# Small constant tiles allocated before the activation tile in a two-layer hybrid decoder trunk

## The chip, the core and the metric

The kernel runs on one core of one Trainium2 chip. The metric is device time in microseconds (us), the median of several executions of the same program. The times below come from one profiled execution where they carry a place in the program, and from three timed runs where they are called runs.

## What is computed

Two residual layers over 512 tokens of width 1024, all in float32. Layer 0 mixes tokens with gated linear attention and block-sparse softmax attention, layer 1 with a gated short convolution and multi-scale pooling. Each layer ends in a wide squared-ReLU MLP, and most of the arithmetic is in the projections and in these two MLPs:

```
def mlp(h, w1, w2):
    a = jax.nn.relu(h @ w1)          # 512x1024 @ 1024x4096
    return (a * a) @ w2              # 512x4096 @ 4096x1024

def reference(x, ...):
    for i in range(DEPTH):           # DEPTH = 2
        h = rmsnorm(x, norm_mix[i])
        x = x + (mix_even(h, ...) if i % 2 == 0 else mix_odd(h, ...))
        h = rmsnorm(x, norm_mlp[i])
        x = x + mlp(h, w1[i], w2[i])
    return x
```

## The kernel before

Channels lie on the 128 partitions, and the 512 tokens run along the free axis of every activation tile. Every large product is done three times: an operand is split into a high and a low part (float32r), and helper `mm3` (lines 124 to 129) issues hi by hi, hi by lo and lo by hi into the same PSUM tile. One such matmul has a stationary operand of 128x128, loaded by its own weight load (PEld in the profile), and a moving operand of 128x512.

Weights arrive as 184 blocks of 128x1024 (512 KB). `block_parts` (lines 101 to 113) fetches a block by SyncE's DMA queue into `raw`, ScalarE casts it to `whi` (line 111), VectorE subtracts to get `wlo` (line 112). The pool `wp` holds four blocks, and three are made ahead of their use. A block feeds 24 matmuls.

Tile `A` (128 partitions, 32 rows of 512 float32r, so 2,048 bytes a row) holds activations: rows 0 to 7 and 8 to 15 the high and low parts of the normed input (called H), rows 16 to 23 and 24 to 31 those of a mixer's output or of an MLP quarter (called O). `t_unit` (lines 131 to 156) reads rows of `A` as the moving operand and weights as the stationary one; the units called qa, ka, ra, wob, woa, u, cg, xc, bg, wo and m1 (all shown as `m<-A` in the MLP) are of this kind. `tok_g` (lines 158 to 172; units kb, qb, vb, va) swaps them: columns of `A` are stationary, weights move.

The MLP (lines 301 to 376) makes its 4096 hidden rows in four quarters of 1024. The quarters 0 and 2 are stored in `A` rows 16 to 31, the quarters 1 and 3 in a tile `E` of 16 rows, which lives in a pool of its own (line 304). `m2(g)` multiplies quarter g by w2, always at line 360 through the same `mm3`, so it reads `A` for g = 0 and 2 and `E` for g = 1 and 3. The order is m1(0), m1(1), m2(0), m1(2), m2(1), m1(3), m2(2), m2(3). One m1(g) or one m2(g) is 4 units x 2 blocks x 24 = 192 matmuls, except the last unit of the program, which is cut finer (lines 332 to 343).

The order of TensorE's work is the order in which the code issues it; in the attention stage of layer 0 a small planner (class `Plan`) interleaves attention steps with pieces of projections by costs written into the kernel. Neither depends on where a tile lies.

The order in which tiles are asked of a pool sets where they lie in a partition. The pool `cp` is opened first (line 60) and its tiles follow each other, rounded up to 32 bytes. The pools behind it start where it ends. These are the byte offsets within a partition that the compiled program has, and their remainders modulo 2,048:

| tile | offset | remainder |
|---|---|---|
| kk, later x | 16,512 | 128 |
| A | 32,896 | 128 |
| cn, vc, g2, eps_c, one_c, ones_r, warm | 98,432 to 106,432 | 128, 1920, 128, 1152, 1184, 1216, 1728 |
| raw, whi, wlo (blocks of 4,096 bytes) | 106,432 to 147,392 | 1984 |
| E | 155,584 | 1984 |
| pwh (pooling weights) | 157,632 | 1984 |
| ph (pooled inputs) | 178,432 and up | 256 |

Of the kernel before, what the change touches and what calls it, by code (L numbers as in the profile page):

```python
# [8 lines left out]
F32R = mybir.dt.float32r  # L9
# [5 lines left out]
P = 128  # L15
S = 512
KT = 8
# [27 lines left out]
def kernel(  # L45
# [14 lines left out]
    cp = ctx.enter_context(tc.tile_pool(name="cp", bufs=1))  # L60
# [4 lines left out]
    )  # L65

    x = None
    kk = cp.tile([P, KT, S], F32R, tag="x", name="kk")
    A = cp.tile([P, 32, S], F32R, name="A")
    cn = cp.tile([P, C_N], F32, name="cn")  # L70
    vc = cp.tile([P, V_N], F32, name="vc")
    g2 = cp.tile([97, 256], F32, name="g2")
# [5 lines left out]
    ones_r = cp.tile([P, P], F32R, name="ones_r")  # L78
    warm = cp.tile([P, 64], F32, name="warm")
    dve.memset(warm, 0.0)  # L80
    ident = cn[:, C_ID : C_ID + P]
    ones = cn[:, C_ONE : C_ONE + P]
    dist = cn[:, C_DIST : C_DIST + S]
# [4 lines left out]
    def col(i, n=1):  # L88
        return vc[:, i : i + n]
# [34 lines left out]
    def mm3(o, w_hi, w_lo, a_hi, a_lo, start, stop, swap=False):  # L124
        if swap:
            w_hi, w_lo, a_hi, a_lo = a_hi, a_lo, w_hi, w_lo
        pe.matmul(o, w_hi, a_hi, start=start, stop=False)  # L127
        pe.matmul(o, w_hi, a_lo, start=False, stop=False)  # L128
        pe.matmul(o, w_lo, a_hi, start=False, stop=stop)  # L129

    def t_unit_g(name, acts):
        o = mm_tile(name)
        n = len(acts)
        for b in range(n // 4):
# [3 lines left out]
            for kk in range(4):  # L138
                k = b * 4 + kk
                for j in range(2):  # L140
                    c = slice(j * P, (j + 1) * P)
                    mm3(o[:, j, :], hi[:, kk, c], lo[:, kk, c], A[:, acts[k][0], :], A[:, acts[k][1], :],
                        k == 0, k == n - 1)
# [14 lines left out]
    def tok_g(name, evac):  # L158
        blocks = []
        for half in range(2):  # L160
            o = mm_tile(f"{name}{half}")
            for k in range(KT):
# [4 lines left out]
                for j in range(2):  # L167
                    t = slice((2 * half + j) * P, (2 * half + j + 1) * P)
                    mm3(o[:, j, :], hi[:, c], lo[:, c], A[:, k, t], A[:, 8 + k, t], k == 0, k == KT - 1, swap=True)
                if k == KT - 1:  # L170
# [1 line left out]
                yield  # L172

    class Plan:
        """Orders the tensor engine's steps: the first listed step whose inputs are due, else a piece of the filler."""

        def __init__(self, banks):
            self.free = {t: [0.0] * n for t, n in banks.items()}
# [76 lines left out]
    def split_h(k, gcol, src, c=slice(0, S)):  # L255
        act.activation(A[:, k, c], src[:, k, c], AF.Copy, scale=col(gcol + k))
        dve.scalar_tensor_tensor(  # L257
            A[:, 8 + k, c], src[:, k, c], col(gcol + k), A[:, k, c].bitcast(F32), op0=ALU.mult, op1=ALU.subtract
        )
# [41 lines left out]
    def mlp(l, nrm, nxt):  # L301
        with ExitStack() as c2:
# [4 lines left out]
            def aslot(f):  # L307
                i = f % 8
                if (f // 8) % 2 == 0:
                    return A[:, 16 + i, :], A[:, 24 + i, :]  # L310
                return E[:, i, :], E[:, 8 + i, :]

            def apair(f):
                i = f % 8
                if (f // 8) % 2 == 0:
                    return A[:, 16 + i : 18 + i, :], A[:, 24 + i : 26 + i, :]
                return E[:, i : i + 2, :], E[:, 8 + i : 10 + i, :]
# [736 lines left out]
```

## Time and profile before

| | |
|---|---|
| three runs | 1119.59, 1121.35, 1121.45 us (median 1121.35) |
| span of the profiled execution | 1119.5 us |
| TensorE matmuls (PE) | 1109.4 us busy, 99%, 5008 matmuls |
| TensorE weight loads (PEld) | 891.2 us, 80% |
| VectorE (DVE) | 556.7 us, 50% |
| ScalarE (ACT) | 405.1 us, 36% |
| GpSimd (POOL) | 103.1 us, 9% |
| mean traffic to and from memory | 93 GB/s |

The profiled execution's own device time is not given beside its span. The span runs from the first to the last instruction; the lowest run is 0.09 us above it and the median 1.85 us. The busy time of PE is no measure of work: matmuls are pipelined, and each record (about 0.39 us) overlaps the next. The time from the start of one matmul to the start of the next is what counts, and it is read from the timeline, where rows carry their start.

### The profile page before, as it was taken

What the parts mean: (1) busy time and instruction counts of PE and PEld (TensorE: products, weight loads), DVE (VectorE), ACT (ScalarE), POOL (GpSimd) and SP (SyncE); (2) the same over time, 40 slices, a digit from 0 to 9 for tenths busy, and PEclk for the clock granted to TensorE, in tenths of its full rate; (3) what the DMA queues carried; (4) which work ended last, traced back from release to release, by engine and by line L of the source; (5) the groups of instructions that cost most, each with busy time, mean ns of one, the idle gap of its engine ahead of it and who ended that gap; (6) DMA issues with size and microseconds to landing.
All of it is one profiled execution on the core that took longest, in us unless ns stands there. A gap on an engine that the chain in (4) does not pass through costs nothing.

```text
span 1119.5 us, 12567 instructions
## 1 busy us (share of the span) xinstructions
PE 1109.4 (99%) x5008; PEld 891.2 (80%) x5008; DVE 556.7 (50%) x774; ACT 405.1 (36%) x554; POOL 103.1 (9%) x110
## 2 busy tenths in 40 slices
PE   9999999999999999999999999999999999999998
PEld 7777778678888888888888888888888888888887
DVE  6887765758544334334325674455443334334321
ACT  5564455535433123223214332244433133133110
POOL 2132312214000000000002100021000000000000
PEclk9999999999999999999999999999999999999999
DMA  7222114113222222223223222232233322232331
GB/s 225 76 76 95 57 43 147 58 57 96 93 95 94 94 94 94 95 96 97 91 100 102 88 94 95 95 94 94 94 94 94 95 94 95 95 94 94 94 112 57
DMA packets 32043, 104.84 MB, mean 94 GB/s; under 512 B 3729, under 2 KB 6258, under 8 KB 31986
## 3 DMA queue, kind: packets, MB, share of 16 engines
q1 hardware_dynamic: 31202, 101.69, 28.0%
q0 software_dynamic: 640, 2.10, 0.6%
q8 instruction: 39, 0.64, 0.2%
q10 hardware_dynamic: 144, 0.26, 0.1%
q14 instruction: 18, 0.15, 0.0%
HBM read 101.94 MB, written 2.10 MB: 93 GB/s over the span
## 4 chain that ended last, share of the span: by engine, by line
PE 93%; DVE 3%; ACT 1%; DMA 1%; POOL 1%; issue 1%; SPq 0%; POOLq 0%; DVEq 0%
PE m L127 21%; PE m L129 21%; PE m L128 21%; PE wo L127 1%; PE wo L129 1%; PE wo L128 1%; DMA raw<-in_w_dram 1%; PE av L690 1%; PE s L642 1%; PE ptp L671 1%; PE s L641 1%; PE va L127 1%; PE cg L129 1%; PE bg L127 1%; PE woa L129 1%; PE woa L128 1%
## 5 line engine op out<-in xcount | busy, mean ns | idle before, releaser
L111 ACT CAST whi<-raw 128x1024 fp32r<-128x1024 f32 (+1 forms) x188 | 193.8, 1031 | 557.6 <-PE m L128 448.0
L112 DVE TENSOR_TENSOR wlo<-raw,whi 128x1024 fp32r<-128x1024 f32 (+1 forms) x188 | 227.7, 1212 | 210.2 <-ACT whi L111 209.9
L128 PE MATMUL m<-A,whi 128*128 128x512 f32 x768 | 303.4, 395 | 0.0
L129 PE MATMUL m<-A,wlo 128*128 128x512 f32 x768 | 303.4, 395 | 0.0
L127 PE MATMUL m<-A,whi 128*128 128x512 f32 x768 | 303.4, 395 | 0.0
L129 PEld LDWEIGHTS m<-A,wlo 128*128 128x128 f32 x768 | 144.1, 188 | 35.1
L128 PEld LDWEIGHTS m<-A,whi 128*128 128x128 f32 x768 | 144.1, 188 | 35.1
L127 PEld LDWEIGHTS m<-A,whi 128*128 128x128 f32 x768 | 144.1, 188 | 35.0
L128 PE MATMUL m<-E,whi 128*128 128x512 f32 (+1 forms) x264 | 101.0, 383 | 0.0
L127 PE MATMUL m<-E,whi 128*128 128x512 f32 (+1 forms) x264 | 101.0, 383 | 0.0
L129 PE MATMUL m<-E,wlo 128*128 128x512 f32 (+1 forms) x264 | 101.0, 383 | 0.0
L287 DVE TENSOR_TENSOR x<-x,m 128x1024 f32<-128x1024 f32 x31 | 37.9, 1222 | 111.9 <-PE m L129 111.9
L326 DVE SCALAR_TENSOR_TENSOR r<-m,rs_n 128x1024 f32<-128x1024 f32 x32 | 39.2, 1225 | 102.3 <-PE m L129 102.3
L268 POOL TENSOR_TENSOR ss_n<-ss_n,sq_n 128x512 f32<-128x512 f32 x21 | 32.8, 1564 | 401.7 <-ACT sq_n L266 401.0
L127 PEld LDWEIGHTS m<-E,whi 128*128 128x128 f32 x264 | 49.6, 188 | 9.8
L129 PEld LDWEIGHTS m<-E,wlo 128*128 128x128 f32 x264 | 49.6, 188 | 9.8
L128 PEld LDWEIGHTS m<-E,whi 128*128 128x128 f32 x264 | 49.6, 188 | 9.7
L327 ACT ACTIVATE r<-r 128x1024 f32<-128x1024 f32 x32 | 34.0, 1063 | 20.3 <-DVE r L326 20.3
L330 DVE TENSOR_TENSOR E<-r,E 128x1024 fp32r<-128x1024 f32 x16 | 19.6, 1225 | 17.2 <-ACT E L329 17.2
L257 DVE SCALAR_TENSOR_TENSOR A<-x,vc,A 128x512 fp32r<-128x512 f32 x24 | 27.3, 1142 | 1.2
L330 DVE TENSOR_TENSOR A<-r,A 128x1024 fp32r<-128x1024 f32 x16 | 19.6, 1224 | 15.1 <-ACT A L329 15.1
L127 PE MATMUL wo<-A,whi 128*128 128x512 f32 x64 | 25.3, 396 | 0.0
(297 smaller groups left out, 1422.8 us busy)
## 6 DMA issues: line engine op xcount, KB each, us to landing
raw<-in_w_dram SPq DMA_DIRECT2D x180, 512.0 KB, 3.4
xin<-in_xT_dram SPq DMA_DIRECT2D x16, 128.0 KB, 3.6
raw<-in_w_dram SPq DMA_DIRECT2D x8, 256.0 KB, 4.1
x<-in_xT_dram POOLq DMA_DIRECT2D x8, 256.0 KB, 5.2
out_dram<-x SPq DMA_DIRECT2D x7, 256.0 KB, 2.0
cn<-in_con_dram SPq DMA_DIRECT2D x1, 736.0 KB, 6.0
pw<-in_poolw_dram ACTq DMA_DIRECT2D x1, 256.0 KB, 2.7
out_dram<-x SPq DMA_DIRECT2D x2, 128.0 KB, 1.7
```

The costliest lines, as they stand in the source:

```text
L111: act.copy(hi[:, c], raw[:, c])
L112: dve.tensor_sub(lo[:, c], raw[:, c], hi[:, c].bitcast(F32))
L127: pe.matmul(o, w_hi, a_hi, start=start, stop=False)
L128: pe.matmul(o, w_hi, a_lo, start=False, stop=False)
L129: pe.matmul(o, w_lo, a_hi, start=False, stop=stop)
L257: dve.scalar_tensor_tensor(A[:, 8 + k, c], src[:, k, c], col(gcol + k), A[:, k, c].bitcast(F32), op0=ALU.mult, op1=ALU.subtract)
L268: (dve if first else pool).tensor_add(ss, ss, sq)
L287: dve.tensor_add(x[:, 2 * n : 2 * n + 2, :], x[:, 2 * n : 2 * n + 2, :], o)
L326: dve.scalar_tensor_tensor(r, o, 0.0, bc2(st["rs"]), op0=ALU.max, op1=ALU.mult)
L327: act.activation(r, r, AF.Square)
L330: dve.tensor_sub(lo, r, hi.bitcast(F32))
L641: pe.matmul(s_[:, :m], qs, kS[p][hh][:, :m], start=True, stop=False)
```

## The change

The two large tiles `kk` and `A` are asked for after the small ones. A docstring gives way to blank lines.

```
@@ -65,8 +65,6 @@
     x = None
-    kk = cp.tile([P, KT, S], F32R, tag="x", name="kk")
-    A = cp.tile([P, 32, S], F32R, name="A")
     cn = cp.tile([P, C_N], F32, name="cn")
     vc = cp.tile([P, V_N], F32, name="vc")
     g2 = cp.tile([97, 256], F32, name="g2")
@@ -78,6 +76,8 @@
     ones_r = cp.tile([P, P], F32R, name="ones_r")
     warm = cp.tile([P, 64], F32, name="warm")
     dve.memset(warm, 0.0)
+    kk = cp.tile([P, KT, S], F32R, tag="x", name="kk")
+    A = cp.tile([P, 32, S], F32R, name="A")
     ident = cn[:, C_ID : C_ID + P]
@@ -172,7 +172,7 @@
     class Plan:
-        """Orders the tensor engine's steps: the first listed step whose inputs are due, else a piece of the filler."""
+
 
         def __init__(self, banks):
```

The small tiles take 5888 + 256 + 1024 + 32 + 32 + 512 + 256 = 8,000 bytes (each rounded up to 32), which is 3 x 2,048 + 1,856. So `A` moves from 32,896 to 40,896 and `kk` (and `x`, which takes its place) from 16,512 to 24,512: both from remainder 128 to remainder 1984. The small tiles move to 16,512 and keep their remainders, since 98,432 - 16,512 = 40 x 2,048. The pool's size is the same, so every other tile stays where it was. The instructions of each of the five engines, and their order, are the same before and after.

## Rows read from the trace of the kernel before

**Rows 1.** The page's part 4: share of the last chain by engine.

```profile
PE 93%; DVE 3%; ACT 1%; DMA 1%; POOL 1%; issue 1%; SPq 0%; POOLq 0%; DVEq 0%
```

**Rows 2.** Waits of TensorE, whole span: total us, times, longest us.

```profile
PE rs_tp L504 <- DVE ss_n L268: 1.8, 1, 1.8
PE o L797 <- DVE st L787: 1.3, 1, 1.3
...
PE ov L811 <- DVE osq L249: 0.8, 2, 0.6
```

**Rows 3.** The page's part 5: weight split by ScalarE and VectorE.

```profile
L111 ACT CAST whi<-raw 128x1024 fp32r<-128x1024 f32 (+1 forms) x188 | 193.8, 1031 | 557.6 <-PE m L128 448.0
L112 DVE TENSOR_TENSOR wlo<-raw,whi 128x1024 fp32r<-128x1024 f32 (+1 forms) x188 | 227.7, 1212 | 210.2 <-ACT whi L111 209.9
```

**Rows 4.** Timeline, TensorE, first matmuls of m2(1), m1(3), m2(2), m2(3), unit u: start us.

```profile
444.97 0.40 PE L127 MATMUL m<-E,whi 128*128 128x512 f32 x1
...
488.51 0.39 PE L127 MATMUL m<-A,whi 128*128 128x512 f32 x1
...
533.31 0.39 PE L127 MATMUL m<-A,whi 128*128 128x512 f32 x1
...
578.11 0.39 PE L127 MATMUL m<-E,whi 128*128 128x512 f32 x1
...
621.65 0.39 PE L127 MATMUL u<-A,whi 128*128 128x512 f32 x1
```

**Rows 5.** Stretches E, A, E: busy (count) of PE, PEld, DVE, ACT, POOL; clock; DMA.

```profile
444.97:488.51 43.54, 43.54 (x193) 36.04 (x192) 15.55 (x13) 10.55 (x11) 0.00 (x0) 1.00 0.29 97
488.51:578.11 89.60, 89.60 (x385) 71.81 (x384) 33.56 (x28) 25.21 (x25) 0.00 (x0) 1.00 0.29 94
578.11:621.65 43.54, 43.54 (x193) 36.04 (x192) 20.21 (x18) 15.56 (x21) 7.63 (x5) 1.00 0.29 97
```

**Rows 6.** Groups by form, TensorE matmuls with A moving, and one with E.

```profile
L127 PE MATMUL m<-A,whi 128*128 128x512 f32 x768 | 303.4, 395 | 0.0
...
L127 PE MATMUL m<-E,whi 128*128 128x512 f32 x248 | 96.5, 389 | 0.0
...
L127 PE MATMUL wo<-A,whi 128*128 128x512 f32 x64 | 25.3, 396 | 0.0
...
L127 PE MATMUL woa<-A,whi 128*128 128x512 f32 x32 | 12.7, 396 | 0.0
...
L127 PE MATMUL qa<-A,whi 128*128 128x512 f32 x16 | 7.0, 438 | 0.0
```

**Rows 7.** Groups by form, weight loads.

```profile
L127 PEld LDWEIGHTS m<-A,whi 128*128 128x128 f32 x768 | 144.1, 188 | 35.0
...
L127 PEld LDWEIGHTS m<-E,whi 128*128 128x128 f32 x264 | 49.6, 188 | 9.8
```

**Rows 8.** Timeline, TensorE, unit qb: A stationary, weights moving.

```profile
41.05 0.39 PE L127 MATMUL qb<-whi,A 128*128 128x512 f32 x1
...
44.49 0.39 PE L127 MATMUL qb<-whi,A 128*128 128x512 f32 x1
```

**Rows 9.** Timeline, TensorE, pooling products between units cg and xc.

```profile
655.71 0.39 PE L127 MATMUL pm<-ph,pwh 128*128 128x512 f32 x1
...
657.09 0.40 PE L127 MATMUL xc<-A,whi 128*128 128x512 f32 x1
...
658.49 0.40 PE L127 MATMUL xc<-A,whi 128*128 128x512 f32 x1
```

**Rows 10.** TensorE by stage: busy (count), clock, DMA share, GB/s.

```profile
27.00:30.00 3.00, 1.16 (x8) 1.00 0.02 7
30.00:34.00 4.00, 4.00 (x14) 0.57 0.50 137
40.00:112.00 72.00, 71.86 (x338) 1.00 0.25 79
112.00:190.00 78.00, 78.00 (x387) 1.00 0.26 87
190.00:240.00 50.00, 47.21 (x328) 1.00 0.14 45
240.00:265.00 25.00, 25.00 (x109) 1.00 0.26 86
265.00:1116.00 851.00, 851.00 (x3693) 1.00 0.29 94
```

**Rows 11.** The page's part 5: VectorE writing the low parts into E and A.

```profile
L330 DVE TENSOR_TENSOR E<-r,E 128x1024 fp32r<-128x1024 f32 x16 | 19.6, 1225 | 17.2 <-ACT E L329 17.2
...
L330 DVE TENSOR_TENSOR A<-r,A 128x1024 fp32r<-128x1024 f32 x16 | 19.6, 1224 | 15.1 <-ACT A L329 15.1
```

More of the change, by code (lines that the diff above doesn't have):

```diff
@@ L67 @@
     x = None
-    kk = cp.tile([P, KT, S], F32R, tag="x", name="kk")
-    A = cp.tile([P, 32, S], F32R, name="A")
     cn = cp.tile([P, C_N], F32, name="cn")
@@ L80 @@
     dve.memset(warm, 0.0)
+    kk = cp.tile([P, KT, S], F32R, tag="x", name="kk")
+    A = cp.tile([P, 32, S], F32R, name="A")
     ident = cn[:, C_ID : C_ID + P]
```

## Prediction

> **What bounds the kernel now.** I read the chain of waits first, then TensorE's own waits, then the timeline. The chain is 93% TensorE [rows 1], so the time is that of one engine's instruction stream, and nearly nothing holds that stream up: the longest waits of the whole span are 1.8, 1.3 and 0.8 us [rows 2]. By stage, TensorE is busy without a break from 240 us to 1116 us and from 112 to 190 us. It is idle for 2.8 us between 190 and 240 us, and for 1.8 us of the three from 27 us on [rows 10]. The two engines that prepare weights need 1.03 and 1.21 us for a block [rows 3], and a block feeds TensorE for 24 x 0.233 = 5.6 us, so supply is no limit. What is left is the rate at which matmuls follow each other. Their busy time does not show it, because records overlap; the distance from start to start does.
>
> That distance is not the same for all matmuls of one form. The reader should take the timeline's five starts [rows 4] and divide:
> - m2(1), moving operand E: 488.51 - 444.97 = 43.54 us over 192 matmuls, 226.8 ns each.
> - m1(3), moving operand A rows 0 to 15: 533.31 - 488.51 = 44.80 us over 192, 233.3 ns each.
> - m2(2), moving operand A rows 16 to 31: 578.11 - 533.31 = 44.80 us over 192, 233.3 ns.
> - m2(3), E again: 621.65 - 578.11 = 43.54 us over 192, 226.8 ns.
>
> m2(1) and m2(2) are the same line, the same weight tiles, the same number of instructions and the same work on VectorE behind them. The granted clock is 1.00 of 2.4 GHz in all three stretches, and TensorE is never idle in them [rows 5]. The weight load takes 188 ns with either tile [rows 7]. The difference is 44.80 - 43.54 = 1.26 us for 192 matmuls, 6.56 ns each. What differs is where the moving operand lies: E has the remainder of the weights (1984), A has another (128). After the change A has E's.
>
> **A second look at the same thing.** Two other kinds of matmul have different pairs of remainders. In unit qb the weights move (1984) and columns of A are stationary (128 plus a multiple of 512): 44.49 - 41.05 = 3.44 us for 15 matmuls, 229.3 ns [rows 8]. In the pooling products the moving tile has 256 and the stationary one 1984 plus a multiple of 512: 657.09 - 655.71 = 1.38 us for 6, 230 ns, while the A matmuls right behind them take 658.49 - 657.09 = 1.40 us for 6, 233.3 ns [rows 9]. Taken modulo 512, stationary minus moving is 0 for E, 192 for both qb and the pooling products, 320 for A. So the distances line up as 0: 226.8, 192: 229 to 230, 320: 233.3. The pooling products have both operands as high up in memory as E, and still are not as fast as E. That speaks for the remainder and against the region of memory.
>
> **The change part by part.** No instruction is added, removed or moved, and no wait, queue or buffer changes; only addresses do. The terms are therefore counts of matmuls times a difference in distance.
>
> 1. *A as moving operand in stretches without a wait.* Each line of `mm3` has 768 matmuls in the MLP, 64 in wo, and 32 each in woa, u, cg, xc and bg (woa's row stands for the five) [rows 6]. That is 3 x (768 + 64 + 160) = 2976 matmuls, all after 240 us, where TensorE is busy in every slice [rows 10]. 2976 x 6.56 ns = 19.5 us. Nothing covers it, and nothing is late next: the E stretches already run at the faster rate with the same supply of weights and the same evacuations.
>
> 2. *A as moving operand in the attention stage.* ra and wob have 32 per line, qa and ka 16 (qa's row stands for both): 3 x 96 = 288 matmuls, worth 1.9 us. Here TensorE fills time between attention steps that wait for VectorE and ScalarE. From 112 to 190 us it never waits, from 190 to 240 us it stands idle for 2.8 us [rows 10], at the steps of lines 797 and 811 [rows 2]. A piece that ends sooner there makes such a wait longer. I take 1.3 us, with bounds 0 and 1.9. If a longer idle time brought the granted clock down, as the 1.8 us before 30 us did (0.57 from 30 to 34 us), that would cost 4 x 0.43 = 1.7 us; I count it in the upper bound only.
>
> 3. *A as stationary operand.* qb, vb and va have 96 matmuls each, 288 in all (kb's run while the inputs still arrive, and I count nothing). Their pair becomes 1984 with 1984, that of E: 288 x (229.3 - 226.8) = 0.7 us, bounds 0 and 288 x 6.56 ns = 1.9.
>
> 4. *Small attention products.* 64 score products (lines 641, 642), 96 on line 690 and 16 gate products also read A as stationary operand, against tiles that keep their places or, for kk, move along. Their pairs change to others, and no row prices them: bounds plus and minus 176 x 6.56 ns = 1.2 us, value 0.
>
> 5. *VectorE, ScalarE and GpSimd on A and x.* VectorE writes the low parts into E in 1225 ns and into A in 1224 ns [rows 11], so the remainder does nothing there; 0. They also lie beside TensorE's stream.
>
> Sum: 19.5 + 1.3 + 0.7 = 21.5 us off the profiled execution, whose span is 1119.5 us, so a span of 1098.0. The median of the runs lies 1.85 us over that span: 1121.35 - 21.5 = 1099.9 us.
>
> **Rivals.**
> - *No change.* E would be fast for another reason than its remainder, and A would stay at 233.3 ns: 1121.35 us. For it: E also lies behind the weights and A before them, and one pair of tiles is a small sample. Against it: the pooling products above, and that A's low and high rows have the same 233.3 ns over 64 KB of addresses. The Trainium skill has a rule that comes out here ("SBUF — State Buffer", section "Who interferes with whom"): TensorE reads its moving operand and its weights through two independent ports, and "PE and ACT never wait on anyone", so that no placement would matter. The trace does not bear that out, since one line with one set of weights goes at 226.8 ns on one tile and 233.3 ns on another.
> - *Half of it.* The distance might depend on more of the address than the remainder, and A would land where qb and the pooling products are, at 229.5 ns: 3264 x 3.83 ns = 12.5 us, 1108.9 us. Against it: E's 16 rows and the weights' several buffers already lie at many different multiples of 2,048, and E's distance is the same in both stretches.
> - *Slower.* Equal remainders would collide: both reads of TensorE start at the same place, each waits for the other, and E escapes only because it lies in a region of its own. From a distance above 233.3 ns in A's matmuls on, the change costs; with the one difference the rows show taken the other way, 3264 x 6.56 = 21.4 us more, 1142.8 us. Against it: E with the weights is just such a pair, and the fastest one seen.
>
> That the change might not do what it says is ruled out by the offsets of the compiled program: A does come to 40,896, remainder 1984.
>
> **How the numbers follow.** The forecast has 0.87, half of it 0.05, no change 0.05, slower 0.03. The forecast's own bounds: at best all 3264 matmuls on A gain (21.4), with 1.9 for term 3 and 1.2 for term 4, 24.5 us, 1096.9; a median as close to its span as the lowest run before would be up to 1.8 us lower still. At worst term 1 alone, less 1.2 and 1.7 us, 16.6 us, 1104.7. I give 1096.0 to 1104.5, which leaves the other cases and a little of the forecast's edges outside. About 0.2% (2.2 us) is what a measurement of this kernel can tell from no change: faster by more than that is the forecast, the half, and none of the others (0.92), the same 0.05, slower 0.03.
>
> **What would show it.** In the changed kernel's timeline m1(3) and m2(2), 384 matmuls on A, should take 2 x 43.54 = 87.1 us instead of 89.6, and every stretch on A should have E's distance; E's own stretches should stay at 43.54. qb should fall from 229.3 to about 226.8 ns. VectorE's and ScalarE's durations, the weight load's 188 ns and the granted clock should not move, and the waits at lines 797 and 811 may grow by some tenths. Wrong would be: A still at 233.3 (the first rival), A at 229 to 230 (the second), A above 233.3 (the third), or A at 226.8 and the time regained in new waits between 190 and 240 us.

## The result, and the profile after

The changed kernel takes 1102.04 us (median of four runs, 1100.57 to 1102.64) against 1121.40 us of the kernel before, measured beside it. The ratio is 0.9826, with a 95% interval of 0.9814 to 0.9838. The forecast was 1099.9 us, in a range of 1096.0 to 1104.5. The profiled execution has a span of 1098.8 us, 20.7 less than the span before; its own time is 1100.57 us, the lowest of its four, 1.47 below their median, so that 20.7 and the medians' 19.4 differ by no more than executions do.

The page's part 1 and the first row of part 4, after the change. TensorE has 92% of the chain (93% before, [rows 1]) and is 99% busy, with 21.8 us less to be busy with. The span fell by 20.7: 1.1 us of idle time came in, 0.8 of it before 30 us, and the first matmul of qb (below) starts no later for it.

```profile
PE 1087.6 (99%) x5008; PEld 889.5 (81%) x5008; DVE 556.4 (51%) x774; ACT 405.4 (37%) x554; POOL 103.2 (9%) x110
...
PE 92%; DVE 4%; ACT 1%; DMA 1%; POOL 1%; issue 1%; SPq 0%; DVEq 0%; POOLq 0%
```

TensorE's waits after the change (total us, times, longest us), which answer to [rows 2]. The waits at lines 797 and 811 did not grow; a small one is new, at tp_q (line 473).

```profile
PE rs_tp L504 <- DVE ss_n L268: 2.0, 1, 2.0
PE o L797 <- DVE st L787: 1.3, 1, 1.3
...
PE ov L811 <- DVE osq L249: 0.8, 2, 0.6
...
PE tp_q L473 <- DVE kn_q L461: 0.3, 1, 0.3
```

TensorE's timeline after the change, at the five places of [rows 4] (the first column is the start in us).

```profile
438.27 0.39 PE L127 MATMUL m<-E,whi 128*128 128x512 f32 x1
...
481.79 0.39 PE L127 MATMUL m<-A,whi 128*128 128x512 f32 x1
...
525.31 0.39 PE L127 MATMUL m<-A,whi 128*128 128x512 f32 x1
...
568.83 0.39 PE L127 MATMUL m<-E,whi 128*128 128x512 f32 x1
...
612.35 0.39 PE L127 MATMUL u<-A,whi 128*128 128x512 f32 x1
```

Each of the four differences is now 43.52 us for 192 matmuls, 226.7 ns from start to start. A has come down from 233.3, E has stayed (226.8 before). The same three stretches by engine, answering to [rows 5], show that little else differs: the clock is 1.00, VectorE's and ScalarE's busy times and the weight loads are as they were to within 0.3 us.

```profile
438.27:481.79 43.52, 43.52 (x193) 36.05 (x192) 15.55 (x13) 10.55 (x11) 0.00 (x0) 1.00 0.29 97
481.79:568.83 87.04, 87.04 (x385) 72.10 (x384) 33.56 (x28) 25.31 (x25) 0.00 (x0) 1.00 0.31 97
568.83:612.35 43.52, 43.52 (x193) 36.05 (x192) 20.21 (x18) 15.57 (x21) 7.63 (x5) 1.00 0.29 97
```

The groups by form, answering to [rows 6, 7, 11]. The record of a matmul on A has gone from 395 to 389 ns, that of one on E is 389 as before, and VectorE writes A's low parts in 1225 ns (1224 before).

```profile
L127 PE MATMUL m<-A,whi 128*128 128x512 f32 x768 | 298.8, 389 | 0.0
...
L127 PEld LDWEIGHTS m<-A,whi 128*128 128x128 f32 x768 | 144.2, 188 | 29.8
...
L127 PE MATMUL m<-E,whi 128*128 128x512 f32 x248 | 96.5, 389 | 0.0
...
L330 DVE TENSOR_TENSOR A<-r,A 128x1024 fp32r<-128x1024 f32 x16 | 19.6, 1225 | 15.1 <-ACT A L329 15.1
```

To see where the time went, four marks on TensorE's timeline: the first matmul of qb, of woa, of the MLP, and the last of the program. First before, then after.

```profile
38.17 0.50 PE L127 MATMUL qb<-whi,A 128*128 128x512 f32 x1
...
242.92 0.40 PE L127 MATMUL woa<-A,whi 128*128 128x512 f32 x1
...
265.32 0.40 PE L127 MATMUL m<-A,whi 128*128 128x512 f32 x1
...
1115.79 0.28 PE L129 MATMUL m<-E,wlo 128*128 128x256 f32 x1
```

```profile
38.06 0.50 PE L127 MATMUL qb<-whi,A 128*128 128x512 f32 x1
...
241.98 0.39 PE L127 MATMUL woa<-A,whi 128*128 128x512 f32 x1
...
263.74 0.39 PE L127 MATMUL m<-A,whi 128*128 128x512 f32 x1
...
1095.05 0.28 PE L129 MATMUL m<-E,wlo 128*128 128x256 f32 x1
```

From woa to the end it took 872.87 us and takes 853.07: 19.8 us less. From qb to woa, with the attention stage in it, it took 204.75 and takes 203.92: 0.8 us less.

### The profile page after: what moved, and what is told of

The parts are those of the page before. It is cut to its first block, busy times and chain, and to the rows that moved or that the text cites. A ratio compares the mean times of both kernels' runs of the same rounds, so it can differ in the third digit from the quotient of the medians.

```text
span 1098.8 us, 12567 instructions
## 1 busy us (share of the span) xinstructions
PE 1087.6 (99%) x5008; PEld 889.5 (81%) x5008; DVE 556.4 (51%) x774; ACT 405.4 (37%) x554; POOL 103.2 (9%) x110
## 4 chain that ended last, share of the span: by engine, by line
PE 92%; DVE 4%; ACT 1%; DMA 1%; POOL 1%; issue 1%; SPq 0%; DVEq 0%; POOLq 0%
PE m L129 21%; PE m L128 21%; PE m L127 21%; PE wo L129 1%; PE wo L128 1%; PE wo L127 1%; DMA raw<-in_w_dram 1%; PE av L690 1%; PE s L642 1%; PE ptp L671 1%; PE s L641 1%; PE va L127 1%; PE va L129 1%; PE va L128 1%; PE xc L129 1%
## 5 line engine op out<-in xcount | busy, mean ns | idle before, releaser
L127 PE MATMUL m<-A,whi 128*128 128x512 f32 x768 | 298.8, 389 | 0.0
L128 PE MATMUL m<-A,whi 128*128 128x512 f32 x768 | 298.8, 389 | 0.0
L129 PE MATMUL m<-A,wlo 128*128 128x512 f32 x768 | 298.8, 389 | 0.0
L326 DVE SCALAR_TENSOR_TENSOR r<-m,rs_n 128x1024 f32<-128x1024 f32 x32 | 39.2, 1225 | 96.8 <-PE m L129 96.7
L330 DVE TENSOR_TENSOR E<-r,E 128x1024 fp32r<-128x1024 f32 x16 | 19.6, 1225 | 17.2 <-ACT E L329 17.2
L330 DVE TENSOR_TENSOR A<-r,A 128x1024 fp32r<-128x1024 f32 x16 | 19.6, 1225 | 15.1 <-ACT A L329 15.1
```

The lines of the kernel that those rows point to most:

```text
L326: dve.scalar_tensor_tensor(r, o, 0.0, bc2(st["rs"]), op0=ALU.max, op1=ALU.mult)
L330: dve.tensor_sub(lo, r, hi.bitcast(F32))
```

## The experiments

The question after the result was not whether A's matmuls had become faster, which the timeline shows, but what of the address decides. Three readings fit: the relation of the two operands' addresses, the moving tile's own remainder, or the region. Ten kernels use one device, an unused tile of 32 to 512 bytes, and are read in one way: by the 384 matmuls on A between m2(1) and m2(3), and by 192 on E beside them.

**w_to_a.** The order of before, and the weights brought to A instead of A to the weights.

```
     dve.memset(warm, 0.0)
+    pad = cp.tile([P, 48], F32, name="pad")       # 192 bytes
```

> The order of before, with an unused tile of 192 bytes behind the constants: A keeps its place and its remainder 128, and the weights, E and all else behind move up by 192 bytes to remainder 128. Theory (the pair decides: stationary minus moving, modulo 512, is 0 again): A and E both at 226.8 ns from start to start, 1102 us. Rival 1 (the moving tile's own remainder decides, 1984 good, 128 bad): A at 233.3 and E at 233.3 too, 1121.4 + 744 x 6.56 ns = 1126.3 us. Rival 2 (the region decides, E is fast because it lies behind the weights): A at 233.3, E at 226.8, 1121 us.

1100.6 us, ratio 0.9808 (0.9789 to 0.9828). On the timeline, the starts of m1(3) on A, m2(3) on E and unit u:

```profile
481.20 0.39 PE L128 MATMUL m<-A,whi 128*128 128x512 f32 x1
...
568.24 0.39 PE L128 MATMUL m<-E,whi 128*128 128x512 f32 x1
...
611.76 0.39 PE L128 MATMUL u<-A,whi 128*128 128x512 f32 x1
```

87.04 us for 384 on A, 43.52 for 192 on E: both 226.7 ns, with A where it was before the change, at remainder 128. So neither A's region nor A's own remainder was at fault, and moving A is not needed: 192 bytes ahead of the weights do the same.

**e_off.** The changed kernel with E alone displaced.

```
+            epad = mp.tile([P, 48], F32, tag="epad", name=f"epad{l}", bufs=1)
             E = mp.tile([P, 16, S], F32R, tag="E", name=f"E{l}", bufs=1)
```

> The changed kernel with 192 unused bytes ahead of E alone, so E is at remainder 128 and the weights and A at 1984. Theory (the pair decides): the matmuls on E go from 226.8 to 233.3 ns, A stays at 226.8: 744 x 6.56 ns = 4.9 us more, 1106.9 us. Rival 1 (own remainder) says the same here. Rival 2 (region): E stays at 226.8, 1102 us.

1106.39 us, ratio 0.9866 (0.9841 to 0.989). The same three places:

```profile
483.15 0.39 PE L127 MATMUL m<-A,whi 128*128 128x512 f32 x1
...
570.21 0.39 PE L127 MATMUL m<-E,whi 128*128 128x512 f32 x1
...
615.01 0.39 PE L127 MATMUL u<-A,whi 128*128 128x512 f32 x1
```

A stays at 87.06 us for 384 (226.7 ns), E rises to 44.80 for 192, 233.3 ns: the slow rate can be moved to the tile that was fast. The span is 4.8 us above that of the changed kernel; 4.9 were expected.

**d512, d320.** The changed kernel with a gap between A and the weights, so that A stays at 40,896 and the weights and E move together:

```
     A = cp.tile([P, 32, S], F32R, name="A")
+    pad = cp.tile([P, 128], F32, name="pad")      # 512 bytes in d512; 80 elements, 320 bytes, in d320
```

> The changed kernel with 512 unused bytes behind A, so weights and E are at remainder 448 and A at 1984: the difference is 512. Theory (modulo 512): A at 226.8 ns, 1102 us, as the changed kernel. Rival 3 (the remainder modulo 2048 has to be equal): A at about 233 ns, about 1121 us, E at 226.8.

> The changed kernel with 320 unused bytes behind A, so that A lies where it does in the changed kernel (40,896, remainder 1984) and the weights and E are at 256: the difference modulo 512 is 320, as in the kernel before. Theory (the pair decides): A at 233.3 ns, E at 226.8, about 1121 us; unit qb at 229.5 ns. Rival 1 (own remainder): A at 226.8, since it keeps 1984. Rival 2 (region, or that kk and A lie behind the constants): 1102 us.

d512: 1100.89 us, A at 226.7 ns. d320: 1120.63 us, A at 233.3 ns. The 384 matmuls run from 482.32 us to the first on E at 569.36 in d512, from 486.51 to 576.11 in d320. An equal remainder modulo 2,048 is sufficient and not necessary, and the slow rate comes back at A's new place with the old difference of addresses. Unit qb, where A is stationary and the weights move, has the same difference with the other sign: in d320 it settles at 228.9 ns, about the 229.5 expected.

**d64, d192, d256.** The same edit with other gaps.

> The changed kernel with 64 unused bytes behind A: stationary minus moving is 64 modulo 512 for A and 0 for E. Theory (the pair's difference modulo 512 decides, and by steps between 0: 226.7, 192: 229.3 and 320: 233.3 ns): A near 227.5 ns, 1102 + 3264 x 0.8 ns = 1104.6 us. Rival (any difference other than a multiple of 512 has the full price): A at 233.3 ns, about 1121 us.

> The changed kernel with 192 unused bytes behind A: the difference for A is 192 modulo 512, as it was for unit qb and for the pooling products in the kernel before. Theory: A at 229.3 ns, 1101.5 + 3264 x 2.6 ns = 1110 us, and qb (difference 320 here) at 233.3 ns. Rival (full price for any difference): A at 233.3 ns, about 1121 us.

> The changed kernel with 256 unused bytes behind A: the difference for A is 256. Theory, by a straight line between 192 and 320: A at 231.3 ns, 1101.5 + 3264 x 4.6 ns = 1116.5 us. Rival (only 256-byte or smaller places matter, not 512): 226.7 ns and 1101.5 us.

1120.6, 1107.17 and 1101.05 us (eight, two and two runs). My scale was wrong here: 64 bytes cost the full price, where I expected an eighth of it (0.8 of 6.6 ns), and 256 bytes cost nothing, where I expected two thirds. The starts of m1(3), m2(3) and unit u in d64, in d192 and in d256:

```profile
486.89 0.39 PE L128 MATMUL m<-A,whi 128*128 128x512 f32 x1
...
576.49 0.39 PE L128 MATMUL m<-E,whi 128*128 128x512 f32 x1
...
620.03 0.39 PE L128 MATMUL u<-A,whi 128*128 128x512 f32 x1
```

```profile
482.97 0.40 PE L128 MATMUL m<-A,whi 128*128 128x512 f32 x1
...
570.88 0.40 PE L128 MATMUL m<-E,whi 128*128 128x512 f32 x1
...
614.45 0.40 PE L128 MATMUL u<-A,whi 128*128 128x512 f32 x1
```

```profile
481.76 0.39 PE L128 MATMUL m<-A,whi 128*128 128x512 f32 x1
...
568.80 0.39 PE L128 MATMUL m<-E,whi 128*128 128x512 f32 x1
...
612.32 0.39 PE L128 MATMUL u<-A,whi 128*128 128x512 f32 x1
```

89.60, 87.91 and 87.04 us for 384 matmuls on A: 233.3, 228.9 and 226.7 ns. E, which moves with the weights, has 226.7 to 226.9 in all three. In d192 unit qb went the other way, as expected: its difference is now 320, that is 64 modulo 256, and two starts in it, 12 matmuls apart, are

```profile
39.83 0.39 PE L128 MATMUL qb<-whi,A 128*128 128x512 f32 x1
...
42.63 0.39 PE L128 MATMUL qb<-whi,A 128*128 128x512 f32 x1
```

2.80 us, 233.3 ns. So with the same two tiles, in d192 and in d320, one role of A is dear and the other is not: the sign of the difference counts, and neither tile's own place decides.

**d128, d32, d224.** Three more gaps, to find the period and the steps in it.

> The changed kernel with 128 unused bytes behind A: stationary minus moving is 128 for A. By the runs so far the difference counts modulo 256 (0, 256 and 512: 226.7 ns; 64 and 320: 233.3; 192: 228.9). Theory A (a period of 256): 128 lies between 64 and 192, so about 231 ns and 1100.5 + 3264 x 4.4 ns = 1115 us. Theory B (a period of 128, and 64 and 192 differ for another reason): 226.7 ns and 1101 us.

> The changed kernel with 32 unused bytes behind A: the difference for A is 32 modulo 256. Theory A1 (the distance rises with the difference from 0 to 64): about 230 ns, 1111 us. Theory A2 (places of 64 bytes count, and 32 is as good as 0): 226.7 ns, 1101 us. Theory A3 (any difference from 0 that small has the full price): 233.3 ns, 1121 us.

> The changed kernel with 224 unused bytes behind A: the difference for A is 224, that is, -32 modulo 256. Theory (192 was cheaper than 64, so the cost falls towards 256): between 226.7 and 228.9 ns, 1101 to 1108 us. Rival (226.7 is not the floor, and a stationary operand read slightly behind the moving one is faster yet): below 226.7 ns, under 1100 us.

1120.52, 1121.57 and 1121.47 us; none differs from before (ratios 0.9991, 1.0006, 1.0003, each interval across 1). All three have A at 233.3 ns in these stretches. Of the theories stated for them only A3 stands. In d128 the rate is not the same everywhere: the 720 matmuls on A ahead of m2(1), from 279.18 to 446.50 us, take 232.4 ns each, where before, d320, d64, d32 and d224 have 233.3 in both stretches. The A stretches of all twelve kernels together, by the address of the stationary operand minus that of the moving one, modulo 256:

| difference modulo 256 | kernels | 384 matmuls on A, us | ns each |
|---|---|---|---|
| 0 | after, w_to_a, e_off, d256, d512 | 87.04 (e_off 87.06) | 226.7 |
| 32 | d32 | 89.60 | 233.3 |
| 64 | before, d64, d320 | 89.60 | 233.3 |
| 128 | d128 | 89.59 | 233.3 (232.4 in the 720 ahead of m2(1)) |
| 192 | d192 | 87.91 | 228.9 |
| 224 | d224 | 89.60 | 233.3 |

**pm_first.** The changed kernel, with the pooling products ahead of unit cg:

```
+                for g in (2 * c, 2 * c + 1):
+                    pool_mm(g)
                 o = t_unit(f"cg{c}", H)
-                for g in (2 * c, 2 * c + 1):
-                    pool_mm(g)
```

> The changed kernel with the pooling products issued ahead of unit cg and not between cg and xc (layer 1, both halves). Theory on why interrupted stretches gain less (a stretch of matmuls has to settle, and needs about ten matmuls after another kind of product before it is at 226.7 ns): xc starts at 226 to 227 ns from its first matmul on, and cg takes over the slow first ten with 224 to 236 ns, mean about 231. Rival (it is a property of xc, or of what VectorE does while it runs): xc's first ten stay at 231 ns on average. The time does not change: 1100 to 1102 us.

1101.48 us, in one run. It was made because of the first matmuls of unit xc. In the changed kernel, right behind the pooling products (whose difference is 192), xc's first, eleventh and twenty-first start at the last three of these; the first row is the first of the six pooling products:

```profile
645.44 0.40 PE L127 MATMUL pm<-ph,pwh 128*128 128x512 f32 x1
...
646.83 0.40 PE L127 MATMUL xc<-A,whi 128*128 128x512 f32 x1
...
649.15 0.39 PE L128 MATMUL xc<-A,whi 128*128 128x512 f32 x1
...
651.42 0.39 PE L129 MATMUL xc<-A,wlo 128*128 128x512 f32 x1
```

xc's first ten take 2.32 us, 232 ns each, the next ten 2.27 us, 227 each. In pm_first xc follows cg without a break, and its first and eleventh start at:

```profile
647.76 0.39 PE L127 MATMUL xc<-A,whi 128*128 128x512 f32 x1
...
650.02 0.39 PE L128 MATMUL xc<-A,whi 128*128 128x512 f32 x1
```

2.26 us for ten, 226 each; and cg's first nine, which run between the pooling products here, are now 224 to 236 ns. In the second half cg comes whole behind them, and its first ten have a mean of 231.7. The slow start follows the interruption, not the unit. Not every interruption does it: in the changed kernel two nps_n products (623.23 and 623.46 us) go between two units u, at 227 ns themselves, and the next u has 227 from its first matmul on.

**rs_late.** The changed kernel with the row sums of line 504 behind kb's last two pieces:

```
-        pj(14)
+        pj(16)
         rp = m_tile("rs_tp", "s")
...
         qk_norm("k", 0)
-        pj(2)
         rs = nrm.rs()
```

> The changed kernel with the four small products of line 504 (the row sums) issued behind unit kb's last two pieces, not ahead of them. In all profiles so far TensorE waits 1.5 to 2.4 us for VectorE at line 504, and in most of them the granted clock then falls for some microseconds. Theory (the wait and the clock behind it cost what the rows show, and the two pieces can fill it): 2 to 4 us less than the changed kernel's 1101 to 1102 us, so 1097.5 to 1099.5 us, and the clock at 1.00 from 30 to 34 us. Rival (the normalisation of kb comes later by as much, and qb's units wait for its PSUM tile): no gain, 1101 to 1102 us. On the question of addresses it says nothing; it is tried since the two together may be better than either kernel.

1107.53 us, ratio 0.989 (0.9868 to 0.9911): 5.5 us worse than the changed kernel. Its longest wait of TensorE:

```profile
PE qb L127 <- DVE kn_k L461: 6.8, 1, 6.8
```

The wait at line 504 is gone, and a longer one stands in its place: qb needs the PSUM tile that the normalisation of kb frees, and this now comes later. The clock was 1.00 from 30 to 34 us, as hoped, but 0.76 over the next six, in which TensorE runs nothing, and 0.80 from 40 to 50. That was the rival, and worse than it said. No version is shown to beat the changed kernel: the medians of w_to_a, d256 and d512 (1100.6 to 1101.05 us) lie within its spread, and none was timed beside it.

## Why the prediction was right, and which terms were not

*What bounds the kernel, and what the two tiles showed.* Right. The distance of 226.8 ns that E had before the change is what A has after it, and no other engine took over.

*Term 1, stretches without a wait: 19.5 us forecast, 19.8 measured* (woa to the end). The small excess is that A came to 226.67 ns, a little under E's 226.77.

*The sum.* 21.5 us were forecast off the span, and 20.7 came. The time of 1102.04 us is 2.1 above the forecast: 0.8 is this, and 1.3 is that the median lay 1.85 us above the profiled span before and 3.2 above it after, which the forecast took as fixed.

*Terms 2 and 3, attention stage and A as stationary operand: 1.3 + 0.7 us forecast, 0.81 + 0.36 measured, of which 0.8 was left.* The sum was mis-sized, and not for the reason that I had allowed for: the waits at lines 797 and 811 did not grow. Adding up, from qb to woa, what each unit takes from the start of a matmul to the start of the next, qa, ka, ra and wob fell by 0.81 us and qb, vb and va by 0.36. The other products took 0.34 us more, more than half of it at tp_q with its new wait. So term 2 brought 2.8 ns a matmul and not 6.56. The pieces of projections between attention steps are mostly 6 to 12 matmuls long, about as long as a stretch needs to settle. Two pieces show it, the second and the last matmul of one of ka (12) and of one of wob (6), first before, then after.

```profile
113.88 0.40 PE L128 MATMUL ka<-A,whi 128*128 128x512 f32 x1
...
116.21 0.40 PE L129 MATMUL ka<-A,wlo 128*128 128x512 f32 x1
...
219.52 0.39 PE L128 MATMUL wob<-A,whi 128*128 128x512 f32 x1
...
220.45 0.39 PE L129 MATMUL wob<-A,wlo 128*128 128x512 f32 x1
```

```profile
113.41 0.39 PE L128 MATMUL ka<-A,whi 128*128 128x512 f32 x1
...
115.70 0.39 PE L129 MATMUL ka<-A,wlo 128*128 128x512 f32 x1
...
218.71 0.39 PE L128 MATMUL wob<-A,whi 128*128 128x512 f32 x1
...
219.63 0.40 PE L129 MATMUL wob<-A,wlo 128*128 128x512 f32 x1
```

In the piece of 12, ten distances fall from 233 to 229 ns; in the piece of 6, four fall from 232.5 to 230. Over all 31 pieces of 6 in these four units the mean of these four is 233.0 before and 230.7 after; in the one piece of 24 (wob) the same distances come to 227.8. The gain grows with the length of the piece. With A stationary, qb's settled distance did fall about as forecast, from 228.9 (229.3 by the rounded starts of [rows 8]) to 226.7 ns, 2.72 us for 12 matmuls in the timeline after:

```profile
41.62 0.39 PE L127 MATMUL qb<-whi,A 128*128 128x512 f32 x1
...
44.34 0.39 PE L127 MATMUL qb<-whi,A 128*128 128x512 f32 x1
```

Of the 0.6 us that 2.2 ns would give on 288 matmuls, the breaks of qb, vb and va left 0.36.

*Term 4, small attention products: value 0.* Right as a size: added up in the same way, the score products take 0.05 us more, those of line 690 and the gate products the same to 0.01. No run shows a price per difference for them.

*Term 5, the other engines: nothing.* Right, by the stretches and groups above.

*The second look.* The conclusion (the relation of the two addresses, not the region) was right and w_to_a shows it, but the scale under it was not. I took the differences modulo 512 and saw distances that rise from 0 through 192 to 320. They count modulo 256, where 320 is 64, and do not rise in order: 32, 64, 128 and 224 have the full price, and 192 a third of it: (228.9 - 226.7) / (233.3 - 226.7). The three values seen before the change fitted a line by chance. One of them was hardly a value: the pooling products' 230 ns is that of six matmuls that had not settled. After the change the two tiles have the same places, and the six take 646.83 - 645.44 = 1.39 us, 232 ns each.

*The rivals.* No change, for which the Trainium skill's rule spoke ("SBUF — State Buffer", section "Who interferes with whom": two independent ports, TensorE never waits), is refuted by the result and by e_off, where 192 bytes ahead of E slow TensorE by 6.6 ns a matmul. What fails is the step from independent ports to a placement that costs nothing; whether the loss arises at a port or behind it, no run shows. The half would have needed a difference such as d192's, which keeps two thirds of the gain. Slower did not come: equal places are the fast ones, in all five kernels that have them on A.

## What to carry to other kernels

Where TensorE is busy without a break, compare start-to-start distances of matmuls of one form on different tiles; the busy share, 99% before and after, hides a difference that the timeline shows at once (and the records' means, 395 and 389 ns, hint at). Where such a pair differs, look at the offsets of the two operands' tiles: here a multiple of 256 bytes between stationary and moving operand was worth 6.6 ns of 233 on each 128x512 float32r matmul, and a pad of 192 bytes earned all of it. Expect less where other products interrupt the stream every few matmuls.

## What the runs showed of the hardware

The distance depends on the difference of the operands' addresses modulo 256 bytes, to the nearest 32 bytes tried, and 192 is a better place than its neighbours; why, no run tells. A stretch keeps a memory of what was before it: in xc ten matmuls pass before it settles, at distances from 224 to 236 ns, on E before the change three to five. At a difference of 128 there are two steady rates, 232.4 ns over 720 matmuls on A and 233.3 over the 384 behind an E stretch; what chooses between them is not shown. In most profiles the granted clock fell near 30 us, at or behind the wait of line 504 (1.5 to 3.9 us), to a mean of 0.50 to 0.73 of 2.4 GHz from 30 to 34 us, that is, to the level of 1.2 GHz for part or all of them, but in d320, d64 and d192 it stayed at 1.00 with waits of 1.6 to 2.0 us; their qb began 1.6 to 1.9 us sooner than that of the changed kernel. The kernel before varies so by itself: in executions with a mean clock of 1.000 its span was 1117.4 to 1118.2 us, in the others 1118.8 to 1122.9. Spans of single profiles of this program therefore differ by 2 us and more for a cause other than addresses, and the stretches above are the better measure.
